# Conditioning vectors of a diffusion trunk: which groups go through TensorE as rows, which are summed on VectorE, and when

## The chip, the core and the metric

The kernel runs on one core of a Trainium2 chip. The core has TensorE (PE, matrix products), VectorE (DVE), ScalarE (ACT), GpSimd (POOL) and SyncE (SP, which issues most of the DMAs). Each engine works through its own list of instructions in order; semaphores make one engine wait for another. The metric is the device time of one execution in microseconds (us), as the median of several.

## The reference, cut to what matters

One layer of a trunk over 2048 latent rows with a context of 256 rows, both 1024 wide. All in float32.

```
ada   = silu(c)     @ w_ada + b_ada        # 6 x 1024 numbers for the latent rows
ada_c = silu(c_ctx) @ w_ada + b_ada        # the same for the context
sh1, sc1, g1, sh2, sc2, g2 = split(ada);   csh1, csc1, ... = split(ada_c)
hc = rmsnorm(ctx) * norm_mix * (1 + csc1) + csh1        # context, 256 rows
(final forward and backward states of a gated recurrence) from hc @ w_in[:, :1536]
h  = rmsnorm(x)   * norm_mix * (1 + sc1)  + sh1         # latent, 2048 rows
o  = token_mixers(h @ w_in, starting from those states)
x  = x + g1 * (o @ w_out);  h2 = modulate(rmsnorm(x), sh2, sc2)
x  = x + g2 * conv_ffn(h2);  return rmsnorm(x)
```

What matters here is the beginning: 2048 of the 6144 conditioning columns (shift sh1 and scale sc1) are needed, for the latent stream and for the context, before anything can be modulated. The others come later in the kernel, and the change doesn't touch them.

## The kernel before, in words

Activations are kept transposed, features on the 128 partitions and positions along the free axis, in 8 blocks of 128 features (`NK` = 8). To keep float32 accuracy, a product is made from a high and a low part of each operand: `split` copies to float32r on ScalarE (line 120) and subtracts on VectorE or GpSimd (line 121), and three products go into one PSUM bank (`mm3`).

**Conditioning.** `w_ada` has one shift and one scale per feature, 1024 columns each. They are cut in four groups of 512: groups 0 and 1 are the lower and upper half of the shift, groups 2 and 3 those of the scale. Index `w` is 0 for the latent stream, 1 for the context. Two ways of working a group out stand side by side:
- as rows: `ada_products` multiplies the two columns of `cs2` (silu of c and of c_ctx) with a 128x512 piece of `w_ada`, eight times into one bank (2 partitions x 512); `ada_columns` adds the bias on VectorE, and transposes the result to columns, 4 x (128 x 2).
- as sums: `ada_sums` runs on VectorE, acc = w_ada piece x scalar + acc over all 128 partitions, eight times for each `w`; a product with a matrix of ones (line 65, tile `acc` as the stationary operand) then adds over the partitions and transposes at once.

Before, groups 0, 2 and 3 are rows, group 1 is summed for both `w`, two accumulators by turns. `put_ada` writes the columns into `s1` (shift) and `a1` (norm_mix x (1 + scale)), at lines 286 and 288.

**Context and first banks.** The two context tiles (128 x 1024) are squared on ScalarE and scaled on VectorE (`x_square`, `x_scale`), transposed on TensorE into four PSUM banks (`pct`), and modulated block by block: `ctx_mod` takes scale and shift on VectorE from PSUM (line 232), the high part on ScalarE, the low part on GpSimd (blocks 0 to 3) or VectorE (4 to 7). All this stands inside `tc.manual_schedule()`, where the written order is the order on every engine. Behind it a planner orders the instructions by its own estimates.

`run_banks` then makes column blocks of `w_in`: a bank is 8 x 3 products of one 128-column block (`hi`, `lo`, split from `raw`) with 256 context columns (`chl`, `cll`) or 512 latent ones (`xh`, `xl`). Two split weights are held at a time, three raw ones. PSUM has three buffers for such banks (tag "pj"). Of a head's three context banks two are forget gates, whose `sink` applies two sigmoids on ScalarE (lines 514, 515) into the tile `cS` or `cf`, and one is the value (line 555). Between products `slot()` runs steps that have fallen due in two pumps, `hg_q` and `bg_q`. `bg_q` starts with `x_start`: squares of four latent tiles (line 221), their scaling (line 227), and `x_first`, which transposes and modulates 512 rows in 8 blocks (line 232, high part line 120, low part line 121 by turns on GpSimd and VectorE), twice. The tiles `xl` and `xh` take the memory in which the conditioning weights (`wa`) lay.

The planner's result around the change: six context banks (two heads), then banks over the latent rows and the other context banks, mixed.

Of the kernel before, what the change touches and what calls it, by code (L numbers as in the profile page):

```python
# [72 lines left out]
def tile_trunk(ctx, tc, x, c, cx, c_ctx, w_ada, b_ada, norm_mix, norm_ffn, w_in, hg_norm, sgu_g, sgu_b,  # L73
# [104 lines left out]
    with es1:  # L178
# [13 lines left out]
        def bank(tag):  # L192
            return ps.tile([P, 512], F32, tag=tag, name=tag, bufs={"pj": 3, "sc": 2, "mi": 3}[tag])
# [55 lines left out]
        acc = ph.tile([P, 2, 512], F32, tag="S", name="acc")  # L249
        G.memset(acc, 0.0)  # L250

        def load_ada(g, qs=(0, 1)):

            for q in (qs,) if isinstance(qs, int) else qs:
                t = wa[g // 2][:, 4 * (g % 2) + 2 * q:4 * (g % 2) + 2 * q + 2, :]
                wts[g, q] = t.rearrange("p a (b e) -> p (a b) e", e=512)
                ld(wts[g, q], wv[:, 4 * q:4 * q + 4, g * 512:(g + 1) * 512])

        def load_bias(g, tag):
            rows[g] = pm.tile([2, 512], F32, tag=tag, name="rows", bufs=2)  # L260
            ld(rows[g], b_ada[0:1, g * 512:(g + 1) * 512].broadcast_to([2, 512]))
# [6 lines left out]

        def ada_columns(g):
            V.tensor_add(rows[g], rows[g], pa.pop(g)[:2, :])  # L270
            pv = bank("pj")
            for j in range(4):
                T.transpose(pv[:, 2 * j:2 * j + 2], rows[g][:, j * P:(j + 1) * P], ident[:2, :2])
            put_ada(g, [pv[:, w:8:2] for w in range(2)])

        def ada_sums(k0, k1):
            for k in range(k0, k1):
                for w in range(2):
                    V.scalar_tensor_tensor(out=acc[:, w, :], in0=wts[1, k // 4][:, k % 4, :], scalar=cs2[:, k, w:w + 1],
                                           in1=acc[:, w, :], op0=ALU.mult, op1=ALU.add)  # L280

        def put_ada(g, cols):
            sl = slice(4 * (g % 2), 4 * (g % 2) + 4)
            for w in range(2):
                if g < 2:
                    V.tensor_copy(s1[:, w, sl], cols[w])
                else:
                    V.scalar_tensor_tensor(out=a1[:, w, sl], in0=cols[w], scalar=1.0, in1=nmix[:, sl],
                                           op0=ALU.add, op1=ALU.mult)
# [4 lines left out]
        def ctx_mod(k, eng):  # L294
            x_mod(pct[k // 2][:, (k % 2) * 256:(k % 2) * 256 + 256], 1, k, chl[:, k, :], cll[:, k, :], CTX, eng)
# [4 lines left out]
        with tc.manual_schedule():  # L300
# [3 lines left out]
            vr = pm.tile([50, P], F32, tag="gu", name="vr", bufs=2)  # L304
            for a, n, r0 in ((norm_mix[0], 8, 0), (norm_ffn[0], 8, 8), (hg_norm[0], 4, 16), (sgu_g[0], 4, 20),
                             (sgu_b[0], 4, 24), (conv_b[0], 22, 28)):
                S.dma_start(vr[r0:r0 + n, :], a.rearrange("(r p) -> r p", p=P))
            load_bias(2, "ot")
            for q in range(2):
                load_ada(0, q)  # L310
                load_ada(1, q)
            load_bias(0, "ot")
            for w in range(2):
                ld(acc[0:1, w, :], b_ada[0:1, 512:1024])
            load_bias(3, "vv")
            load_ada(3)
            load_raw((0, CTX))
# [5 lines left out]
            pv = bank("sc")  # L323
            T.transpose(pv[:, :50], vr, ident[:50, :50])
            V.tensor_copy(vec, pv[:, :50])
            ada_products(2, 1)
            ada_columns(2)
            x_scale(xc, ss, keep=lambda i: i)
            ada_sums(0, 4)
            ada_products(0, 0)  # L330
# [4 lines left out]
            load_raw((HW, CTX))  # L335
            ada_products(0, 1)
            ada_columns(0)
            ada_sums(4, 5)
            for k in range(4):
                ctx_mod(k, G)  # L340
                if k == 1:
                    ada_sums(5, 6)
            ada_products(3, 0)
# [3 lines left out]
            ada_sums(6, 8)  # L347
            nxt[0, CTX] = split_w((0, CTX), G)
            ada_products(3, 1)
            pz = bank("pj")  # L350
            for w in range(2):
                for j in range(4):
                    o = 2 * (4 * w + j)
                    T.matmul(pz[:, o:o + 2], acc[:, w, j * P:(j + 1) * P], ones[:, :2], start=True, stop=True)
            ada_columns(3)
            put_ada(1, [pz[:, 8 * w:8 * w + 8:2] for w in range(2)])
            for k in range(4, NK):
                ctx_mod(k, V)
            nxt[HW, CTX] = split_w((HW, CTX), V)
        xl = p1.tile([P, NK, TH], F32R, tag="xl", name="xl", align_bytes=AL)  # L360
        xh = p1.tile([P, NK, TH], F32R, tag="xh", name="xh", align_bytes=AL)

        def x_first(g0, xs):
            for k in range(NK):
# [116 lines left out]
        def run_banks(banks, peek=None):  # L481
# [3 lines left out]
            for i, (col, n0, n, sink, pre) in enumerate(banks):  # L485
# [10 lines left out]
                pj = bank("pj")  # L496
                sl = slice(n0, n0 + n)
                for k in range(NK):
# [99 lines left out]
        def marked(g, what):  # L598
# [7 lines left out]
                (view(cf, 0, [[CTX, 2], [1, CTX]]), view(cf, 2 * CTX, [[CTX, 2], [1, CTX]]), view(cb, CTX, [[1, CTX]]))]  # L606
        bg_q.add(marked(x_start(), "x0b"))
# [1135 lines left out]
```

## Time and profile before

| | us |
|---|---|
| median of 3 runs | 2509.79 (2508.38 to 2512.24) |
| the profiled execution | 2513.77 |
| its span, first to last instruction | 2511.9 |
| TensorE busy | 2440.4 (97% of the span) |
| VectorE busy | 1796.9 (72%) |
| mean granted clock of TensorE | 0.993 |

How to read the lines that follow: a group or timeline line gives start and length (us), engine, line of the kernel, operation, out<-in, shapes, a count (x8: eight merged into one entry), and in brackets the idle time before it with what ended it. PEld is the loading of TensorE's stationary operand, "SPq" the issue of DMAs by SyncE.

### The profile page before, as it was taken

What the parts mean: (1) busy time and instruction counts of PE and PEld (TensorE: products, weight loads), DVE (VectorE), ACT (ScalarE), POOL (GpSimd) and SP (SyncE); (2) the same over time, 40 slices, a digit from 0 to 9 for tenths busy, and PEclk for the clock granted to TensorE, in tenths of its full rate; (3) what the DMA queues carried; (4) which work ended last, traced back from release to release, by engine and by line L of the source; (5) the groups of instructions that cost most, each with busy time, mean ns of one, the idle gap of its engine ahead of it and who ended that gap; (6) DMA issues with size and microseconds to landing.
All of it is one profiled execution on the core that took longest, in us unless ns stands there. A gap on an engine that the chain in (4) does not pass through costs nothing.

```text
span 2511.9 us, 32816 instructions
## 1 busy us (share of the span) xinstructions
PE 2440.4 (97%) x11859; PEld 2015.6 (80%) x11859; DVE 1796.9 (72%) x2375; ACT 964.2 (38%) x1606; POOL 1062.2 (42%) x871
## 2 busy tenths in 40 slices
PE   7999999899999999999999999999999999999998
PEld 4787888788888888788788888878788888888786
DVE  5866875645766766465798877759999983767775
ACT  2554334433444443354443333333333333332252
POOL 1344232332343443100688788777777860000002
PEclk8999999999999999999999999999999999999999
DMA  8356446573354323768822222562222238835544
GB/s 293 97 185 189 133 128 193 175 250 126 106 176 143 118 97 104 257 211 255 298 86 80 88 88 87 176 227 83 84 90 92 91 122 341 298 118 182 182 151 172
DMA packets 307838, 400.13 MB, mean 159 GB/s; under 512 B 33105, under 2 KB 216137, under 8 KB 304605
## 3 DMA queue, kind: packets, MB, share of 16 engines
q1 hardware_dynamic: 304420, 397.30, 47.5%
q8 instruction: 94, 1.54, 0.3%
q10 hardware_dynamic: 3257, 0.75, 0.1%
q14 instruction: 67, 0.55, 0.1%
HBM read 288.85 MB, written 109.13 MB: 158 GB/s over the span
## 4 chain that ended last, share of the span: by engine, by line
PE 38%; DVE 7%; DMA 2%; POOL 2%; issue 2%; ACT 1%; SPq 0%; POOLq 0%; DVEq 0%; ACTq 0%
PE up L65 24%; PE dn L65 14%; DVE dn L1331 3%; DMA sT<-wd 1%; POOL Al L121 1%; DVE edges L1336 1%; DVE gp L1407 0%; DMA raw<-in_w_up_dram 0%; DVE mhl L121 0%; POOL raw L1158 0%; DMA yl<-yd 0%; DVE odd L1611 0%; POOL fl L1154 0%; DMA xn<-cv 0%; DVE tl L121 0%
## 5 line engine op out<-in xcount | busy, mean ns | idle before, releaser
L1331 DVE SCALAR_TENSOR_TENSOR dn<-gp,taps,dn 128x1024 f32<-128x1024 f32 x352 | 448.2, 1280 | 20.7 <-ACT dn L1328 17.4
L121 POOL TENSOR_TENSOR Al<-raw,Ah 128x512 fp32r<-128x512 f32 x264 | 344.9, 1313 | 99.7 <-ACT Ah L120 93.1
L65 PE MATMUL pj<-xh,whi 128*128 128x512 f32 x896 | 363.8, 406 | 0.5 <-ACT xh L120 0.5
L65 PE MATMUL dn<-th,mhl 128*128 128x512 f32 x1120 | 353.0, 396 | 5.2 <-DVE odd L1677 4.8
L65 PE MATMUL pj<-xl,whi 128*128 128x512 f32 x896 | 350.7, 392 | 1.8 <-DVE xl L121 1.1
L65 PE MATMUL pj<-xh,wlo 128*128 128x512 f32 x896 | 350.8, 391 | 1.0 <-DVE wlo L121 1.0
L65 PE MATMUL up<-xah,Ah 128*128 128x512 f32 x704 | 277.1, 394 | 1.7 <-ACT Ah L120 1.7
L65 PE MATMUL up<-xah,Al 128*128 128x512 f32 x704 | 276.4, 393 | 2.4 <-POOL Al L121 2.4
L65 PE MATMUL up<-yl,Ah 128*128 128x512 f32 x704 | 274.6, 390 | 2.1 <-DMA yl<-yd 2.1
L120 ACT CAST Ah<-raw 128x512 fp32r<-128x512 f32 x264 | 160.5, 618 | 295.3 <-PE up L65 238.8
L65 PEld LDWEIGHTS dn<-th,mhl 128*128 128x128 f32 x1120 | 212.0, 189 | 54.8 <-issue 4.6
L121 POOL TENSOR_TENSOR wlo<-raw,whi 128x1024 fp32r<-128x1024 f32 x56 | 136.8, 2442 | 250.3 <-ACT whi L120 228.2
L113 POOL TENSOR_SCALAR rs<-ss 128x2 f32<-128x2 f32 (+1 forms) x16 | 8.2, 512 | 535.4 <-ACT jk L1603 368.9
L65 PE MATMUL dn<-tl,mhl 128*128 128x512 f32 x560 | 220.9, 394 | 0.0
L65 PE MATMUL up<-yh,Ah 128*128 128x512 f32 x528 | 208.2, 395 | 0.0
L65 PE MATMUL up<-yh,Al 128*128 128x512 f32 x528 | 206.9, 392 | 0.0
L65 PE MATMUL up<-xal,Ah 128*128 128x512 f32 x528 | 205.6, 389 | 0.0
L65 PEld LDWEIGHTS pj<-xh,wlo 128*128 128x128 f32 x896 | 168.3, 188 | 37.2 <-DVE wlo L121 1.7
L65 PEld LDWEIGHTS pj<-xh,whi 128*128 128x128 f32 x896 | 168.8, 188 | 33.9 <-issue 3.5
L65 PEld LDWEIGHTS pj<-xl,whi 128*128 128x128 f32 x896 | 168.9, 188 | 32.9 <-DVE xl L121 2.1
L65 PE MATMUL dn<-wo,o 128*128 128x512 f32 x768 | 183.1, 394 | 1.5 <-DVE nt L673 0.9
L65 PEld LDWEIGHTS dn<-wo,o 128*128 128x128 f32 x768 | 141.9, 188 | 31.2 <-issue 1.1
(320 smaller groups left out, 4673.5 us busy)
## 6 DMA issues: line engine op xcount, KB each, us to landing
raw<-in_w_up_dram SPq DMA_DIRECT2D x88, 512.0 KB
mr<-m SPq DMA_DIRECT2D x85, 512.0 KB
raw<-in_w_in_dram SPq DMA_DIRECT2D x68, 512.0 KB
sT<-wd SPq DMA_DIRECT2D x88, 256.0 KB
raw<-in_w_ada_dram SPq DMA_DIRECT2D x32, 512.0 KB
m<-cv SPq DMA_DIRECT2D x22, 544.0 KB
raw<-in_w_down_dram SPq DMA_DIRECT2D x22, 512.0 KB
wd<-raw SPq DMA_DIRECT2D x22, 512.0 KB
```

The source lines that it names most:

```text
L65: return self.engine.matmul(out, lhsT, rhs, **kw)
L113: keep(G.tensor_scalar(out=r[:, :n], in0=ss, scalar1=scale, scalar2=bias, op0=ALU.mult, op1=ALU.add))
L120: keep(S.copy(hi, raw))
L121: (eng or G).tensor_sub(lo, raw, hi.bitcast(F32))
L1331: V.scalar_tensor_tensor(out=cr, in0=gt[:, t // 3:t // 3 + RH, t % 3:t % 3 + GW], scalar=taps[:, t * NF + f:t * NF + f + 1], in1=cr, op0=A ...
L1336: V.scalar_tensor_tensor(out=e[:, 0, :], in0=gt[:, 1, t % 3:t % 3 + GW], scalar=taps[:, t * NF + f:t * NF + f + 1], in1=e[:, 0, :], op0=AL ...
```

## The change

Groups 0 and 2, the lower halves, stay rows. Groups 1 and 3, the upper halves, are both summed on VectorE, each with an accumulator of its own, first for the context alone. The bias no longer comes in by loads of its own; it is loaded with the other vectors (`vr`, 66 rows now) and added as columns (`bc`). The row of a group goes from PSUM to SBUF on ScalarE (`ada_rows`). TensorE makes the first half of group 0 ahead of the transposes of group 2. Context blocks 0 to 3 are modulated on ScalarE from PSUM, blocks 4 to 7 on both engines; the low part is always VectorE's. The first weight is split early, on VectorE, and the first context bank gets its products of blocks 0 to 3 (`ctx_products`) before the sums of group 3; `run_banks` goes on with block 4. The latent stream's sums of groups 1 and 3 are put off: six steps (`last_sums`) become due in `hg_q` from 3 us on at 2.5 us distance, and `x_first` runs what is left of them before its first block. The accumulators take the memory tagged "S" (later `cS`) and "bst" (later `cb`).

```diff
+        acc = {1: ph.tile([P, 2, 512], F32, tag="S", name="acc1"),
+               3: view(ph.tile([P, NCH + 1, P], F32, tag="bst", name="acc3"), 0, [[512, 2], [1, 512]])}
...
+        def ada_rows(g, tag):
+            rows[g] = pm.tile([2, 512], F32, tag=tag, name="rows", bufs=2)
+            S.copy(rows[g], pa.pop(g)[:2, :])
...
-        def ada_sums(k0, k1):
+        def ada_sums(g, w, k0, k1):
             for k in range(k0, k1):
-                for w in range(2):
-                    V.scalar_tensor_tensor(out=acc[:, w, :], in0=wts[1, k // 4][:, k % 4, :], scalar=cs2[:, k, w:w + 1],
-                                           in1=acc[:, w, :], op0=ALU.mult, op1=ALU.add)
+                s_ = V.scalar_tensor_tensor(out=acc[g][:, w, :], in0=wts[g, k // 4][:, k % 4, :], scalar=cs2[:, k, w:w + 1],
+                                            in1=acc[g][:, w, :], op0=ALU.mult, op1=ALU.add)
+                if w == 0:
+                    pin(s_)
+        def ada_ones(g, w, to, o):
+            for j in range(4):
+                T.matmul(to[:, o + 2 * j:o + 2 * j + 2], acc[g][:, w, j * P:(j + 1) * P], ones[:, :2], start=True, stop=True)
+            put_ada(g, to[:, o:o + 8].rearrange("p (j u) -> p u j", u=2)[:, :1, :], w, w + 1)
...
+            dst = (s1, a1)[g // 2][:, w0:w1, sl]
+            V.tensor_add(dst, cols, view(bc, 4 * g, [[0, w1 - w0], [1, 4]]))
+            if g > 1:
+                V.tensor_mul(dst, dst, view(vec, sl.start, [[0, w1 - w0], [1, 4]]))
...
+        def ctx_mod(k):
+            pt = pct[k // 2][:, (k % 2) * 256:(k % 2) * 256 + 256]
+            sc, sh = a1[:, 1, k:k + 1], s1[:, 1, k:k + 1]
+            fl = pm.tile([P, 512], F32, tag="sig", name="xfl", bufs=2)
+            if k < 4:
+                S.activation(fl[:, :CTX], pt, AF.Identity, bias=sh, scale=sc)
+                S.copy(chl[:, k, :], fl[:, :CTX])
+            else:
+                S.activation(chl[:, k, :], pt, AF.Identity, bias=sh, scale=sc)
+                V.tensor_scalar(out=fl[:, :CTX], in0=pt, scalar1=sc, scalar2=sh, op0=ALU.mult, op1=ALU.add)
+            V.tensor_sub(cll[:, k, :], fl[:, :CTX], chl[:, k, :].bitcast(F32))
+        def ctx_products(c, ks):
+            hi, lo, _ = nxt[c, CTX]
+            pj = opened[c, CTX]
+            for k in ks:
+                mm3(pj[:, :CTX], hi[:, k, :], lo[:, k, :], chl[:, k, :], cll[:, k, :], k == 0, False)
...
+            load_ada(0)
+            load_raw((0, CTX))
+            load_ada(1)
             load_ada(3)
-            load_raw((0, CTX))
+            load_raw((HW, CTX))
...
             ada_products(2, 1)
+            ada_rows(2, "ot")
+            x_scale(xc, ss, keep=lambda i: i)
+            ada_products(0, 0)
             ada_columns(2)
...
+            nxt[0, CTX] = split_w((0, CTX), V)
...
             ada_products(0, 1)
+            ada_rows(0, "ot")
+            ada_sums(1, 1, 0, 8)
             ada_columns(0)
+            ada_ones(1, 1, small, 256)
+            opened[0, CTX] = bank("pj")
             for k in range(4):
+                ctx_mod(k)
+            ctx_products(0, range(4))
...
+            ada_sums(3, 1, 0, 8)
+            ada_ones(3, 1, small, 288)
             for k in range(4, NK):
-                ctx_mod(k, V)
+                ctx_mod(k)
             nxt[HW, CTX] = split_w((HW, CTX), V)
+        last_sums = []
+        for g in (1, 3):
+            last_sums += [lambda g=g, k=k: ada_sums(g, 0, k, k + 4) for k in (0, 4)]
+            last_sums.append(lambda g=g: ada_ones(g, 0, bank("mi"), 0))
...
         def x_first(g0, xs):
+            while last_sums:
+                sums_now()
...
+        for i in range(6):
+            hg_q.later(sums_now, 3.0 + 2.5 * i)
```

80 lines of the change are left out of this document (26 added, 54 removed).

## The prediction

> **What bounds the kernel now.** I read the page first, then busy time by stage, the engines' timelines up to 110 us, and who waits for whom.
>
> ```profile
> PE 2440.4 (97%) x11859; PEld 2015.6 (80%) x11859; DVE 1796.9 (72%) x2375; ACT 964.2 (38%) x1606; POOL 1062.2 (42%) x871
> 0.00:20.00 20.00, 12.08 (x28) 2.36 (x29) 2.61 (x7) 3.79 (x6) 2.69 (x11) 1.00 0.90 332
> 20.00:40.00 20.00, 14.29 (x50) 4.53 (x48) 16.78 (x24) 2.57 (x5) 6.92 (x5) 0.96 1.05 377
> 40.00:60.00 20.00, 18.76 (x104) 17.46 (x104) 10.29 (x23) 10.53 (x21) 0.24 (x2) 0.70 0.52 168
> 60.00:80.00 20.00, 16.50 (x117) 14.18 (x115) 18.62 (x28) 13.94 (x25) 11.25 (x6) 1.00 0.42 124
> 80.00:100.00 20.00, 17.44 (x103) 13.68 (x102) 17.81 (x30) 7.26 (x15) 6.33 (x6) 1.00 0.24 64
> 49.90:104.90 55.00, 47.62 (x299) 39.81 (x298) 46.89 (x73) 31.05 (x59) 19.59 (x13) 0.97 0.38 115
> ```
>
> Columns of a stage: its length, then busy time of PE, PEld, DVE, ACT, POOL, the granted clock, the DMA share, GB/s. TensorE bounds the whole (97%), so an edit in the first stage counts only by how far it shifts the moment from which TensorE no longer stops. Up to 40 us TensorE waits for data and conditioning; from 60 to 100 us it idles again, 3.5 and 2.6 us in the two stages, and there VectorE is the full engine (18.6 and 17.8 of 20). From 49.9 to 104.9 VectorE is busy 46.9 of 55 us. The waits say what its 8.1 us of idle are:
>
> ```profile
> DVE wlo L121 <- ACT whi L120: 4.7, 3, 2.7
> DVE xfl L232 <- POOL xl L121: 1.3, 2, 0.9
> DVE xg L227 <- POOL rs L115: 0.9, 1, 0.9
> DVE xl L121 <- ACT xh L120: 0.7, 1, 0.7
> DVE xfl L232 <- PE mi L69: 0.5, 1, 0.5
> ```
>
> ```profile
> 50.10 1.23 DVE L121 TENSOR_TENSOR wlo<-raw,whi 128x1024 fp32r<-128x1024 f32 x1 [0.52 <-ACT whi L120]
> 61.05 2.74 DVE L227 TENSOR_SCALAR xg<-xg,rs 128x1024 f32<-128x1024 f32 x4 [0.91 <-POOL rs L115]
> 64.84 1.52 DVE L232 TENSOR_SCALAR xfl<-mi,a,s 128x512 f32<-128x512 f32 x2
> 104.21 0.69 DVE L121 TENSOR_TENSOR xl<-xfl,xh 128x512 fp32r<-128x512 f32 x1
> 108.45 0.28 PE L65 MATMUL pj<-ch,whi 128*128 128x256 f32 x1
> ```
>
> So one VectorE stream runs from the second weight split (50.10) over normalising and modulating the first 1024 latent rows to their last low part (104.21, done 104.90), and TensorE enters the next context bank 3.6 us behind it, at 108.45. In both programs as built, the instruction order of every engine is the same from about there on. The change is worth what it moves that point.
>
> **The change: the front.** These rows price it.
>
> ```profile
> 12.72 3.60 PE L65 MATMUL pj<-wa,cs 128*2 128x512 f32 x8
> 20.95 1.53 PE L69 MATMUL mi<-ident,raw 128*128 128x128 f32 x12
> 22.84 3.60 PE L65 MATMUL pj<-wa,cs 128*2 128x512 f32 x8
> 28.92 7.03 PE L65 MATMUL pj<-wa,cs 128*2 128x512 f32 x16
> 39.51 3.54 PE L65 MATMUL pj<-ones,acc 128*128 128x2 f32 x16 [3.56 <-POOL wlo L121]
> 269.52 0.95 PE L65 MATMUL mi<-ones,acc 128*128 128x2 f32 x8
> 22.56 5.39 DVE L279 SCALAR_TENSOR_TENSOR acc<-wa,cs,acc 128x512 f32<-128x512 f32 x8 [3.48 <-DMA acc<-in_b_ada_dram]
> 327.66 3.10 DVE L885 SCALAR_TENSOR_TENSOR acc<-raw,cs,acc 128x512 f32<-128x512 f32 x4
> 34.36 5.71 DVE L279 SCALAR_TENSOR_TENSOR acc<-wa,cs,acc 128x512 f32<-128x512 f32 x4
> 36.07 2.79 POOL L121 TENSOR_TENSOR wlo<-raw,whi 128x1024 fp32r<-128x1024 f32 x1
> 33.77 0.40 ACT L120 CAST ch<-xfl 128x256 fp32r<-128x256 f32 x1 [1.84 <-DVE xfl L232]
> L1205 ACT ACTIVATE fl<-up,s,a x56: 543/558/568, 1043.5 to 1205.6; 128x256 f32<-128x256 f32 x56
> ```
>
> Removed: 7.03 us of TensorE products for group 3 (28.92), at a place where TensorE then waits 3.56 us anyway, and POOL's share in the front, which stretched VectorE's last four sums to 5.71. Added: sixteen more sums (32 instead of 16) and sixteen more transposing products with ones.
>
> The sums alternated between two accumulators before: 8 in 5.39, 0.67 each. Now eight in a row add to the same accumulator. A chain like that is the row at 327.66: 4 in 3.10, 0.775 each, so eight cost 6.2. The Trainium skill (VectorE: DVE Perf Modes, "The DRAIN you can't avoid") says that a semaphore between chained VectorE instructions costs nothing extra; by that eight would again take 5.4, and my total would be 2.1 us lower. The trace differs, and it decides.
>
> TensorE: group 2 ends at 16.3 as before; group 0's first half (3.6, the length of its second at 22.84) now follows at once, to 19.9; columns 0.3; sixteen context transposes 1.9 (20.95 to 22.84) to 22.1; second half to 25.7, ScalarE's copy of the row and its transposes to 26.9. VectorE: group 2's columns at 20.8, the first weight's low part 1.2, then group 1's sums 22.0 to 28.2. The loads, in slices of 2.5 us:
>
> ```profile
> GB/s 6 228 402 417 391 393 407 410 408 409 392 315 306 402 411 370 261 377 13 0 5 286 275 130 328 29 143 181 105 0 37 173 206 4 0 7 0 0 175 124
> 48.14 0.54 DVE L232 TENSOR_SCALAR xfl<-sc,a,s 128x256 f32<-128x256 f32 x1
> 47.80 0.42 DVE L121 TENSOR_TENSOR cl<-xfl,ch 128x256 fp32r<-128x256 f32 x1 [0.47 <-ACT ch L120]
> ```
>
> On SP's queue now come group 2 and the context (3.1 MB), group 0 (2.1), the first weight (0.5), group 1 (2.1) and group 3 (2.1). The slices add up to 7.9 MB at 23 us and 10 MB at 28.5; a transfer lands about 1 us behind its bytes. So group 1's second half is there at 24, its fifth sum starts at 25; group 3's is needed after 32. The second and third weights wait for the two context tiles (free at 22.1) behind group 3, which delays nothing, as the queue is that long anyway; the latent rows follow and land before 40, long before their squares. The five bias loads taken off SP and the one put on ScalarE's queue (SP's second load of group 2 now waits on an early small one) hide behind that stream, which keeps at 400 GB/s; if they don't, the front slips by a small load's landing, some 2 us. Then ScalarE modulates four blocks: 0.56 for scale and shift from PSUM (L1205's form, same shape) and 0.40 for the cast, chained 0.93 with VectorE's subtraction behind: 3.7 + 0.5. It starts at 28.4 if it waits for its own shift columns alone, or at 29.5 if also for group 1's (eight products with ones, warm, 0.95): VectorE is free at 32.6 or 33.7. Group 3's sums: 6.2, to 38.8 or 39.9. The twelve early products of the first context bank lie beside this. The ones products find TensorE idle for five microseconds; after 3.56 us of idle the row at 39.51 shows 0.22 each, so 1.8 instead of 0.95; columns 0.4: 41.05 or 42.1. Four more blocks, scale-and-shift 0.54 and subtraction 0.42 chained on VectorE, 3.75. **The second weight split starts at 44.8 or 45.9, instead of 50.10.** I take the middle, 45.3: a lead of 4.8 us.
>
> **The change: the stage behind it.** Sixteen sums (groups 1 and 3 for the latent stream) now sit in the VectorE stream. In the built order they stand 4, 3, 1 (group 1) and 8 singly (group 3), before the first latent modulation. A chain of four costs 3.1, one of three 2.3, those between other instructions 0.7: 3.1 + 2.3 + 0.7 + 8 x 0.7 = 11.7, and three small column writes 0.4. The stream gets 46.9 + 12.1 = 59.0 busy.
>
> Its idle time, with times for the early case: before, 4.7 was waiting for ScalarE's weight casts, which wait for a bank to end. Now
>
> ```profile
> 51.38 0.39 PE L65 MATMUL pj<-ch,wlo 128*128 128x256 f32 x1 [0.76 <-DVE wlo L121]
> 55.22 0.32 PE L65 MATMUL pj<-ch,whi 128*128 128x256 f32 x1
> 50.22 0.38 ACT L514 ACTIVATE cS<-pj 128x256 f32<-128x256 f32 x1 [0.15 <-issue]
> 50.77 1.06 ACT L221 ACTIVATE xjk<-xg 128x1024 bf16<-128x1024 f32 x1
> 59.33 0.19 ACT L221 ACTIVATION_READ_ACCUMULATOR xjk<-xg 128x1 f32 x1
> 59.67 0.20 POOL L113 TENSOR_SCALAR rs<-xss 128x4 f32<-128x4 f32 x1 [20.82 <-ACT xjk L221]
> 61.86 0.33 PE L69 MATMUL mi<-ident,xg 128*128 128x128 f32 x1 [1.17 <-DVE xg L227]
> ```
>
> bank two runs from 46.05; 18 products at half clock take 3.8 (51.38 to 55.22), the bank ends at 50.4. VectorE has split bank three and done four sums by 50.25 and waits 1.3 for the next cast.
> The new wait lies in the tags: the accumulator of group 1 has taken buffer S, in which the first context gates are kept. Sink cS therefore waits until the ones products have read it, behind bank four. Banks one and two stay in PSUM, banks three and four share the one buffer left. ScalarE's queue holds behind that sink the other context sinks (0.38 each) and all four squares of the latent rows (1.06 and 0.19 to read the sum). Bank four ends at 56.65, ones at 57.9 (VectorE waits 1.05 for them), first square at 58.6 instead of 50.77. With sinks between, squares end at 63.9, POOL's rstd takes 1.5 (59.52 to 61.05 before), normalising at 65.5 instead of 61.05 (VectorE waits 0.6). Group 3's sums end at 69.9; TensorE has stood since bank six ended at 64.4, so ones are cold again, 1.8; VectorE waits 1.5; first latent modulation at 73.3 instead of 64.84. Later waits as before, 1.3 for POOL, 0.7 and 0.5 for casts and transposes: 2.6. Idle: 1.3 + 1.05 + 0.6 + 1.5 + 2.6 = 7.05.
>
> Sum: 45.3 + 59.0 + 7.05 = 111.35, against 104.90: **+6.4 us**. A second way, by the stages: first modulation +8.5 (early case), less two weight splits (2.4) now behind it, no POOL split among them: +5 to +7. I take +6.2. TensorE has 2.75 us of latent transposes more to do behind 74 us than before (five groups of four at about 0.55), but enough idle there: 2.6 in the stage from 80 alone. The profiled execution is 2513.77 for a span of 2511.9, 4.0 above the median of 2509.79: it would become 2520.0, and the median **2516**.
>
> Bounds: the lead of the front is at least 4.2 (45.9) and at most 6.4 (unchained sums 1.6 less, 0.67 each); added work at least 16 x 0.67 = 10.7 and at most 16 x 1.43 (34.36) = 22.9, were POOL beside every sum; it is beside few, so I stay near the first. The idle could be 2.6 (all new waits covered) to 10.
>
> **Rivals.** (a) The idle swallows more: new waits overlap with sums that the stream had to do anyway, idle 3.5, chain spacing 0.67. Then -1 to +4, 2512. For: the scheduler spread the sums. Against: each wait named has nothing ahead of it in VectorE's order.
> (b) Faster: the latent modulation isn't what TensorE needs next, and the lead stays. Bank two's split products start 4.9 earlier (51.38 to 46.5) and the stall of 1.17 at 61.86 vanishes: -6, 2504. It decides if the stream ends by 99.9, that is if VectorE's idle of 8.1 takes in nearly all twelve added. Against: 4.7 of it came at bank ends, in pieces under 2.7, and the latent squares start eight late.
> (c) POOL beside the sums: the fourth split of POOL and its power (2.4 and 1.06) fall at 64 to 70, among the last sums, and each costs VectorE about its own length, as 34.36 against 36.07 shows (5.71 instead of 3.10, beside 2.79). In the sum this replaces a like collision before; where it comes on top, +3.5: 2519.5. The Trainium skill (SBUF — State Buffer, "Who interferes with whom") has it as an exclusive lock between VectorE with two SBUF inputs and GpSimd: the second blocks for the whole instruction. The trace agrees: 2.6 more beside 2.79.
>
> **Numbers.** 0.2% is 5.0 us, about what a measurement of this kernel tells from no change. Forecast, +4 to +8.5: 0.50, of which 0.42 lies above 5.0. (a) 0.27, (b) 0.08, (c) and worse 0.15. Slower 0.42 + 0.15 = 0.57, same 0.08 + 0.27 = 0.35, faster 0.08. Range 2509 to 2521.5: it leaves out (b) and the ends of (a) and (c), about 0.17.
>
> **What would show it.** Right: second weight split near 45; first cS sink behind 56; TensorE idle for about 5 us before the second set of ones near 64 to 70; first modulation of latent rows behind 70; the bank of 108.45 near 114.5. Wrong: latent squares that start before 55, sums that hide in VectorE's idle, or a first modulation before 67; in the front, a split at 42 or at 48.

## The result and the profile after

The changed kernel takes 2522.42 us (median, 2516.81 to 2524.07) where the kernel before takes 2509.79 in the same series: ratio 1.0042, 95% interval 1.0028 to 1.0056. That is slower, by some 10.5 us as the ratio has it (7 to 14); the two medians lie 12.6 apart. The profiled execution took 2516.81 us for a span of 2515.0. It is the fastest of its series, so the two spans are no measure of the change; the shift of matching instructions is.

Busy time by stage of the changed kernel, with the columns of the table before (length, PE, PEld, DVE, ACT, POOL, granted clock, DMA share, GB/s); the last row is the VectorE stream, from the second weight split to the last low part of the latent rows:

```profile
0.00:20.00 20.00, 13.04 (x25) 2.30 (x25) 1.94 (x6) 4.62 (x8) 3.57 (x12) 1.00 0.89 315
20.00:40.00 20.00, 12.33 (x58) 7.68 (x56) 15.16 (x25) 4.95 (x10) 0.00 (x0) 0.75 1.06 392
40.00:60.00 20.00, 16.96 (x99) 15.10 (x98) 15.47 (x25) 8.36 (x13) 0.00 (x0) 0.74 0.65 206
60.00:80.00 20.00, 14.06 (x77) 13.31 (x78) 17.40 (x28) 9.30 (x20) 5.99 (x4) 0.68 0.39 114
80.00:100.00 20.00, 17.48 (x94) 14.16 (x92) 15.13 (x27) 11.51 (x23) 6.83 (x6) 0.89 0.09 27
46.31:114.02 67.71, 56.71 (x313) 48.39 (x314) 57.60 (x93) 30.53 (x58) 17.18 (x13) 0.84 0.31 94
```

TensorE, the bound of the whole, idles longer: it is busy for 14.06 us between 60 and 80, against 16.50 before, and at a granted clock of 0.68 against 1.00. Along the timeline of the changed kernel:

```profile
46.31 1.23 DVE L121 TENSOR_TENSOR wlo<-raw,whi 128x1024 fp32r<-128x1024 f32 x1
59.73 1.06 ACT L221 ACTIVATE xjk<-xg 128x1024 bf16<-128x1024 f32 x1
66.76 2.74 DVE L227 TENSOR_SCALAR xg<-xg,rs 128x1024 f32<-128x1024 f32 x4 [0.91 <-POOL rs L115]
68.83 2.87 POOL L121 TENSOR_TENSOR wlo<-raw,whi 128x1024 fp32r<-128x1024 f32 x1 [2.11 <-ACT whi L120]
69.42 2.83 DVE L283 SCALAR_TENSOR_TENSOR acc<-wa,cs,acc 128x512 f32<-128x512 f32 x1
73.26 1.84 PE L65 MATMUL mi<-ones,acc 128*128 128x2 f32 x8 [5.86 <-DVE acc L283]
76.55 1.52 DVE L232 TENSOR_SCALAR xfl<-mi,a,s 128x512 f32<-128x512 f32 x2
113.35 0.67 DVE L121 TENSOR_TENSOR xl<-xfl,xh 128x512 fp32r<-128x512 f32 x1
117.92 0.28 PE L65 MATMUL pj<-ch,whi 128*128 128x256 f32 x1
```

The second weight split starts 3.8 us earlier than before (46.31, 50.10), the first square of the latent rows 9.0 later (59.73, 50.77), the first latent modulation 11.7 later (76.55, 64.84), the stream's last low part 9.1 later (113.35, 104.21), and TensorE enters the bank that serves as landmark 9.5 later (117.92, 108.45). Behind the landmark the order of instructions is the same in both kernels. The later end is made ahead of it.

### The profile page after: what moved, and what is told of

It is laid out like the page before. It is cut to its first block, busy times and chain, and to the rows that moved or that the text cites. A ratio compares the mean times of both kernels' runs of the same rounds, so it can differ in the third digit from the quotient of the medians.

```text
span 2515.0 us, 32819 instructions
## 1 busy us (share of the span) xinstructions
PE 2442.0 (97%) x11855; PEld 2023.4 (80%) x11855; DVE 1804.0 (72%) x2392; ACT 968.1 (38%) x1612; POOL 1053.4 (42%) x867
```

## The experiments

Four theories were told apart. A: the deferred sums' own VectorE time, ahead of the first latent modulation, sets it. B: the accumulator's buffer, which holds up the cS sink and with it the squares, sets it. C: POOL's split beside a sum adds about 2 us. D: the front gains or loses it. Each result is read at the landmark (108.45 before, 117.92 after) and by the ratio to the kernel before. The front's end moves by up to 2.5 us between executions of the same front (the second split was at 46.31 in the changed kernel and at 47.98 in a kernel that differs from it only behind that point, and at 48.05 and 50.52 in two kernels that differ only in a buffer; the last section shows what moves it). There is one profile of each kernel. Distances from the second split are therefore the surer reading.

**The sums left out.**

```diff
         for g in (1, 3):
-            last_sums += [lambda g=g, k=k: ada_sums(g, 0, k, k + 4) for k in (0, 4)]
             last_sums.append(lambda g=g: ada_ones(g, 0, bank("mi"), 0))
```

> The changed kernel with the 16 deferred sums left out: the latent rows' upper shifts and scales are then the bias alone (that part of the computation is left out); their products with the ones stay. The landmark is the context bank that ended at 108.45 us before and at 117.92 us after. Theory A (the sums' own VectorE time sets the later end): they are busy 11.9 us in the changed kernel, and the one stretched by POOL 2.1 of it, so the landmark comes 10 to 12 us earlier, at 106 to 108, and the time is at or below the kernel before. Theory B (the wait of the cS sink for the accumulator's buffer sets it): the products with the ones still stand behind bank four only if bank four's time holds them; without sums they can run at once, so the squares of the latent rows start near 51 instead of 59.73 and the first latent modulation comes near 65: the landmark is near 106 to 108 too. The two differ in the next two runs. Theory D (the front): the second split stays at 46.3 us, and the landmark must be earlier than the kernel before by at most the 3.8 us of lead that the front has: not below 104.6.

Ratio 1.0002 (0.9993 to 1.0011), landmark 108.18. The slowdown is gone. But the products with the ones had nothing left to wait for and were planned into the front, where VectorE waited for them (1.91 and 1.85 us); the second split came at 49.57 instead of 46.3. So this run shows that the sums are the cause, and not what the front's lead is worth. (The sums are busy for 14.03 us in the changed kernel; the 11.9 of the expectation leaves out the 2.1 by which one of them was stretched.)

**The accumulator in another buffer, all sums kept.**

```diff
-        acc = {1: ph.tile([P, 2, 512], F32, tag="S", name="acc1"),
+        acc = {1: view(ph.tile([P, NCH + 1, P], F32, tag="fs", name="acc1"), 0, [[512, 2], [1, 512]]),
```

> The changed kernel with the group-1 accumulator in the memory of tag fs (used by a later bank) instead of tag S, so that the cS sink no longer waits for the products with the ones. All sums stay. Theory A: only idle time is gained, the sums still stand ahead of the first latent modulation on VectorE; first sink near 53 instead of 59.2, squares near 53 instead of 59.73, but the first modulation (76.55) not before 73, and the landmark at 115 to 116.5 (1.5 to 3 us earlier than 117.92), the time 1.005 to 1.002 of the kernel before. Theory B: the squares, the rstd and the modulation all come 6 to 8 us earlier, landmark at 110 to 112, the time within 0.1% of the kernel before. The stretched sum beside POOL's split (theory C) may go or stay, worth up to 2.1 us.

Ratio 1.0033 (1.0021 to 1.0046), landmark 118.44. From the timeline of this run:

```profile
49.40 1.06 ACT L221 ACTIVATE xjk<-xg 128x1024 bf16<-128x1024 f32 x1
58.26 2.74 DVE L227 TENSOR_SCALAR xg<-xg,rs 128x1024 f32<-128x1024 f32 x4 [0.91 <-POOL rs L115]
76.27 0.74 DVE L283 SCALAR_TENSOR_TENSOR acc<-wa,cs,acc 128x512 f32<-128x512 f32 x1
79.99 1.66 DVE L232 TENSOR_SCALAR xfl<-mi,a,s 128x512 f32<-128x512 f32 x2 [0.60 <-PE mi L69]
60.00:80.00 20.00, 9.82 (x68) 9.44 (x69) 17.61 (x33) 4.18 (x8) 2.45 (x1) 0.80 0.45 132
```

The squares start 10.3 us earlier than in the changed kernel and the rows are normalised 8.5 earlier, and nothing comes of it, not even the 1.5 to 3 us that theory A allowed: the last sum still starts at 76.27, the modulation at 79.99, and TensorE is busy for 9.82 of the 20 us ahead of that. The gate levels (VectorE's short steps on `cS` and `tot`, lines 497 and 504), released early, only took VectorE's turns between the sums. With sixteen sums deferred, theory B falls: its wait was covered by the sums.

**Both edits at once.** The two diffs above.

> Both edits at once: the 16 deferred sums left out (the latent rows' upper shifts and scales are then the bias alone) and the accumulator in the other memory. If the buffer costs nothing without the sums, this agrees with the run without sums alone within 0.5 us at the landmark; theory B expects a further gain of 2 us or more over it. Either way this is what the front alone is worth: the second split at 46.3 us against 50.10 is 3.8 us of lead, so the landmark is at 104.7 to 106 if the lead is kept and near 108 if the stretch behind swallows it.

Ratio 1.0006 (0.9997 to 1.0015), landmark 108.46, second split 49.99: as without the sums alone. Without sums the buffer costs nothing.

**No sums and no products with ones.**

```diff
-        for g in (1, 3):
-            last_sums += [lambda g=g, k=k: ada_sums(g, 0, k, k + 4) for k in (0, 4)]
-            last_sums.append(lambda g=g: ada_ones(g, 0, bank("mi"), 0))
+        for t in (s1, a1):
+            V.tensor_copy(t[:, 0, 4:8], t[:, 1, 4:8])
...
```

> The changed kernel without the deferred sums and without their products with the ones; the latent rows take the context's upper shifts and scales instead (their own are left out: two copies of four columns in their place). Unlike the run that only left the sums out, nothing is put into the front, so the second split should stand at 46.5 to 47 us. The runs so far: first latent modulation 64.84 before (second split 50.10), 64.52 without the sums (49.57), 64.72 with rows for group 3 (49.02), 76.55 in the changed kernel and 79.99 with the other buffer; landmark 108.45, 108.18, 108.58, 117.92, 118.4. Theory A (what stands ahead of the first latent modulation sets the landmark, and the deferred sums stand there): the modulation near 62 to 63, landmark 104.5 to 106, that is 12 to 13 us earlier than the changed kernel, and the time some 3 us below the kernel before. If the stretch between swallows the front's lead (TensorE's banks at half clock set the squares, and these the modulation): modulation at 64.5, landmark at 108, the time of the kernel before.

Ratio 1.0004 (0.9994 to 1.0013), second split 47.97, first modulation 63.90, landmark 107.81. Against the changed kernel this prices the sixteen sums together with their products with the ones, for which VectorE waits 1.2 and 1.7 us there: from second split to landmark 59.84 us here, 71.61 there, 11.8 more. It also shows that a lead of the front mostly does not come through: 2.13 us at the split (the front was expected a microsecond earlier, at 46.5 to 47), 0.64 at the landmark. The front loses nothing by itself, so theory D falls as the cause of the later end.

**Eight sums deferred instead of sixteen.** Group 3 goes back to rows on TensorE; the latent column of group 1 alone is deferred.

```diff
-            ada_sums(3, 1, 0, 8)
-            ada_ones(3, 1, small, 288)
+            ada_products(3, 0)
+            ada_products(3, 1)
+            ada_rows(3, "ot")
+            ada_columns(3)
...
-        for g in (1, 3):
+        for g in (1,):
             last_sums += [lambda g=g, k=k: ada_sums(g, 0, k, k + 4) for k in (0, 4)]
```

> Group 3 as rows on TensorE (behind the products of blocks 0 to 3, second split near 49), and only the latent column of group 1 deferred: 8 sums instead of 16, the accumulator in the same buffer as in the changed kernel. 16 deferred sums moved the landmark from 107.8 (none deferred) to 117.9. If every deferred sum costs its own time (0.78 us of VectorE): half of it, landmark 112.5 to 113.5, time 1.002. If VectorE's idle time in the bank stage (5.65 us of it between 50 and 58 us in the kernel before) takes the first 8 and only what is over costs: landmark 108.5 to 110, time 1.000 to 1.001. The cS sink behind the products with the ones puts the squares at 56 to 58; if these set the modulation: modulation 68 to 70, landmark 111 to 112.

Ratio 1.0031 (1.002 to 1.0042), landmark 115.80, above all that was expected: more than half the cost for half the sums. The squares started at 62.12 and the first modulation at 74.94. Here the chain over the buffer is the longer one, which the next run tests, with the accumulator in tag "fs".

```diff
-        acc = {1: ph.tile([P, 2, 512], F32, tag="S", name="acc1")}
+        acc = {1: view(ph.tile([P, NCH + 1, P], F32, tag="fs", name="acc1"), 0, [[512, 2], [1, 512]])}
```

> The run with 8 deferred sums (group 1 alone, group 3 as rows) once more, with the accumulator in the memory of tag fs, so that the cS sink does not wait for the products with the ones. With the accumulator in tag S it had its squares at 62.12 us, its first latent modulation at 74.94 and its landmark at 115.80, more than half of what 16 sums cost. With all 16 sums the other buffer gained nothing (118.44 for 117.92). If with 8 sums it is the buffer that sets the end: squares near 51, modulation 65 to 67, landmark 108.5 to 110.5, time 1.000 to 1.001. If the sums' own VectorE time does, here too: modulation 70 to 72, landmark 112.5 to 114.5, time 1.002.

Ratio 1.0025 (1.0016 to 1.0035), squares 52.86, modulation 71.27, landmark 114.45, but with the second split at 50.52 instead of 48.05. From split to landmark it is 63.93 us against 67.75: the buffer is worth 3.8 us. The first modulation waited for the sums now:

```profile
67.62 0.74 DVE L282 SCALAR_TENSOR_TENSOR acc<-wa,cs,acc 128x512 f32<-128x512 f32 x1
69.79 0.95 PE L65 MATMUL mi<-ones,acc 128*128 128x2 f32 x8
70.78 0.16 DVE L295 TENSOR_TENSOR s<-mi,bc 128x4 f32<-128x4 f32 x1 [1.14 <-PE mi L65]
```

So theory B accounts for 3.8 of the 9.4 us that eight sums cost between split and landmark, and for nothing with sixteen, and VectorE's idle time did not take in eight sums either: 63.93 is 5.6 more than the 58.35 of the kernel before. Modulation, landmark and time fall where the sums' own time was expected to put them; measured from the split, both causes show.

**The eighth weight split on VectorE.** POOL's split beside the sums is taken away.

```diff
-            split(hi, lo, raw, eng or (V if w_n[0] < 8 or w_n[0] < 20 and w_n[0] % 2 else G))
+            split(hi, lo, raw, eng or (V if w_n[0] < 9 or w_n[0] < 20 and w_n[0] % 2 else G))
```

> The changed kernel with the eighth split of a weight on VectorE (1.22 us) instead of POOL (2.87 us, which stood beside the one sum that took 2.83 us instead of 0.77). Theory C (the collision): the sum is short again, VectorE gains 2.1 us and gives 1.2 back, so the second products with the ones come near 72.4 instead of 73.26 and the landmark near 117.0; what POOL did elsewhere stays. If nothing waited on that sum: landmark 118 to 119. In neither case is the time told apart from the changed kernel's (1.003 to 1.005 of the kernel before).

Ratio 1.0036 (1.0023 to 1.0048). The sum in question took 0.75 us again instead of 2.83. From split to landmark 70.72 against 71.61: 0.9 less, which is the 2.1 gained minus the 1.2 for the split. Theory C is right in its place and its size, and small; the front was 1.7 us late in this execution, so the landmark itself (118.70) shows nothing.

**The context blocks modulated as before.**

```diff
-                ctx_mod(k)
+                x_mod(pct[k // 2][:, (k % 2) * 256:(k % 2) * 256 + 256], 1, k, chl[:, k, :], cll[:, k, :], CTX, V)
```

(in both loops)

> The changed kernel with the eight context blocks modulated as in the kernel before (VectorE multiplies and adds, ScalarE casts, VectorE subtracts), all else as changed: the ScalarE part of the change undone. A block takes about 1.36 us that way, and VectorE comes to group 3's sums some 2.5 us later: second split near 49 instead of 46.31. If the front's lead never reached the landmark: 117.5 to 119, as in the changed kernel. If it did, with the sums behind it: 120.5 to 121, time 1.005.

Ratio 1.0057 (1.004 to 1.0073), second split 51.16, landmark 123.46, both later than expected. Here the split is 4.85 us later than in the changed kernel and the landmark 5.5: with the sums behind it, a microsecond of the front counted in full in this pair, as it would with VectorE as the bound from the front to the landmark. Of the 4.85, 0.8 is not ScalarE's part: the first products with the ones took 1.84 us in this execution and 1.02 in the changed kernel's. ScalarE's part of the change was thus worth some 4.7 us inside a change that lost 9.5.

**Group 3 as rows, nothing deferred: three orders.** First behind the context's products of blocks 0 to 3:

```diff
-            ada_sums(3, 1, 0, 8)
-            ada_ones(3, 1, small, 288)
+            ada_products(3, 0)
+            ada_products(3, 1)
+            ada_rows(3, "ot")
+            ada_sums(1, 0, 0, 8)
+            ada_columns(3)
+            ada_ones(1, 0, small, 320)
...
```

(In this kernel and the three behind it the deferred steps and group 3's accumulator are taken out as well.)

> Group 3 goes back to rows on TensorE, in the stretch of 29.8 to 39.2 us in which TensorE does little, and VectorE takes the second column of group 1 (8 sums of 0.78 us) in the place of group 3's; no sum is left behind the front. All else is as in the changed kernel. The cold products with the ones ahead of blocks 4 to 7 (1.84 us) are replaced by four transposes; second split near 44.5 us (46.31 after, 50.10 before). Theory A with the lead kept: landmark near 103 (5.5 us earlier than before), time 2504, ratio 0.998. If the stretch behind swallows the lead because its squares or loads come no earlier: landmark 106 to 108, ratio 0.999 to 1.000. Theory D (the front itself costs, ScalarE's and VectorE's turns on the blocks): landmark above 108.

Ratio 0.9998 (0.9989 to 1.0007), second split 49.02, landmark 108.58. The rows ran from 33.97 to 42.33, and VectorE idled 4.07 us for their columns.

Then ahead of those products:

```diff
             ada_columns(0)
+            ada_products(3, 0)
             ada_ones(1, 1, small, 256)
+            ada_sums(1, 0, 0, 8)
+            ada_products(3, 1)
+            ada_rows(3, "ot")
+            ada_columns(3)
+            ada_ones(1, 0, small, 320)
...
```

> Group 3 as rows on TensorE again, but ahead of the context's products (in two halves, the ones of group 1 between them), and VectorE sums both columns of group 1 one after the other; nothing is deferred. In the first form of this edit the rows stood behind the products of blocks 0 to 3 and took 33.97 to 42.33 us, so that the second split was at 49.02. Here the rows end near 36.5, the context's blocks are modulated from about 37.5, and the second split is at 44 to 46.5 us (before 50.10). Theory A with the lead kept: first latent modulation 60 to 62, landmark 103 to 105, the time 3 to 5 us below the kernel before (ratio 0.998 to 0.999). Lead swallowed by the bank stage: landmark 107 to 108.5, ratio 1.000.

Ratio 0.9988 (0.9979 to 0.9997), but second split 49.19 and landmark 108.91, 0.5 us later than before. What the time gained is not to be seen at the landmark, and behind it the order is the same; I don't count it as shown. The next kernel dealt the blocks out in turn:

```diff
             for k in range(4):
                 ctx_mod(k)
+                x_mod(pct[k // 2 + 2][:, (k % 2) * 256:(k % 2) * 256 + 256], 1, k + 4, chl[:, k + 4, :], cll[:, k + 4, :], CTX, V)
...
-            for k in range(4, NK):
-                ctx_mod(k)
```

> As the kernel before this one in the list (rows for group 3 ahead, nothing deferred), with the eight context blocks dealt out alternately: blocks 0 to 3 by ScalarE alone, and between them blocks 4 to 7 by VectorE with ScalarE's cast, as the kernel before has it, so that the two engines never read one PSUM tile at a time. Eight blocks then take about 6 us instead of 8.6 (ScalarE 4 x 0.97 + 4 x 0.41 = 5.5 us; VectorE 4 x 0.55 + 8 x 0.43 = 5.6 us): second split 42 to 44.5. Lead kept: landmark 101 to 103, ratio 0.997 to 0.998. Lead swallowed: landmark 107 to 108.5.

Ratio 1.0007 (0.9997 to 1.0017), second split 49.58, landmark 109.46. The two missed their split by 2.7 and 5.1 us (later than the end of the expected range) through their own order: VectorE waited 4.84 and 3.36 us for the products with the ones ahead of the second column's sums, and in the second of them the blocks waited for each other, 2.25 us a pair. The last form mends both: group 1's second sums ahead of the first ones products, and the blocks one step apart.

```diff
-            ada_ones(1, 1, small, 256)
             ada_sums(1, 0, 0, 8)
+            ada_ones(1, 1, small, 256)
...
+                V.tensor_scalar(out=fl[:, :CTX], in0=pt, scalar1=a1[:, 1, j:j + 1], scalar2=s1[:, 1, j:j + 1], op0=ALU.mult, op1=ALU.add)
+                both[k]()
+                S.copy(chl[:, j, :], fl[:, :CTX])
+                if k < 3:
+                    both.append(ctx_mod(k + 1))
+                V.tensor_sub(cll[:, j, :], fl[:, :CTX], chl[:, j, :].bitcast(F32))
...
```

(`both` holds the low-part subtractions of blocks 0 to 3)

> Rows for group 3 ahead of the context's products and nothing deferred, as in the two runs before, but with their two mistakes of order mended: VectorE's second column of group 1 now stands ahead of the wait for the first products with the ones (it cost 4.84 us of idle time, 29.5 to 34.3), and blocks 0 to 3 on ScalarE and 4 to 7 on VectorE are overlapped by one step, with a buffer of their own, so that a pair takes 1.4 to 1.6 us instead of 2.25. The blocks start near 37.5 and end near 44; second split 43 to 44.5 (before 50.10). So far a second split of 49.57, 49.02, 47.97 and 49.19 gave a landmark of 108.18, 108.58, 107.81 and 108.91: a lead of up to 2.1 us came through by 0.64 at most. If the lead is only lost because these leads were small against the half clock: landmark 103 to 105, time 0.997 to 0.999. If the bank stage sets its own pace (TensorE's matmuls at half clock, 0.21 us each, six banks of 24): first latent modulation 62.5 to 64, landmark 106.5 to 108, time 0.999 to 1.000.

Second split 44.25, landmark 105.51, ratio 0.9993 (0.9982 to 1.0004). The landmark lies between the two expectations, 2.9 us earlier than in the kernel before, half of the front's lead of 5.85. The time is not told from that of the kernel before. What took the other half:

```profile
48.36 1.04 ACT L120 CAST whi<-raw 128x1024 fp32r<-128x1024 f32 x1 [4.14 <-PE pj L65]
49.44 1.22 DVE L121 TENSOR_TENSOR wlo<-raw,whi 128x1024 fp32r<-128x1024 f32 x1 [3.47 <-ACT whi L120]
45.00:50.00 5.00, 5.00 (x24) 5.00 (x25) 1.20 (x3) 1.64 (x4) 0.00 (x0) 0.50 0.38 117
50.00:55.00 5.00, 5.00 (x41) 5.00 (x40) 2.45 (x6) 4.70 (x10) 0.00 (x0) 0.93 0.55 168
```

The timeline rows show the next cast waiting 4.14 us for a bank on TensorE, and VectorE waiting for the cast; the first stage row shows TensorE busy for the whole 5 us, at half clock. When nothing is deferred, the bank stage goes at TensorE's pace, and half or more of an earlier front is lost in waiting.

**All runs by time and landmark.** The ratio times 2510 against the landmark's shift from 108.45:

| kernel | deferred sums | second split | landmark | shift | by the ratio |
|---|---|---|---|---|---|
| before | 0 | 50.10 | 108.45 | 0 | 0 |
| changed | 16 | 46.31 | 117.92 | +9.5 | +10.5 |
| other buffer | 16 | 47.06 | 118.44 | +10.0 | +8.3 |
| split 8 on VectorE | 16 | 47.98 | 118.70 | +10.3 | +9.0 |
| blocks as before | 16 | 51.16 | 123.46 | +15.0 | +14.3 |
| eight sums | 8 | 48.05 | 115.80 | +7.4 | +7.8 |
| eight, other buffer | 8 | 50.52 | 114.45 | +6.0 | +6.3 |
| no sums | 0 | 49.57 | 108.18 | -0.3 | +0.5 |
| no sums, other buffer | 0 | 49.99 | 108.46 | 0 | +1.5 |
| no sums, no ones | 0 | 47.97 | 107.81 | -0.6 | +1.0 |
| rows, first order | 0 | 49.02 | 108.58 | +0.1 | -0.5 |
| rows, second order | 0 | 49.19 | 108.91 | +0.5 | -3.0 |
| rows, blocks in turn | 0 | 49.58 | 109.46 | +1.0 | +1.8 |
| last form | 0 | 44.25 | 105.51 | -2.9 | -1.8 |

The landmark's shift and the time agree within the intervals (about 2.5 to 4 us either way) in every kernel but one: the second order of the rows, whose interval (-5.3 to -0.8) leaves out its landmark's +0.5. The cause of that one is open.

## Why the prediction came out as it did

The direction, the mechanism and the landmark were right; the size was too small, 9.5 us at the landmark for 6.2. The median of 2522.42 lies 0.9 above the range's upper end; 2509.79 times the ratio is 2520.3, inside it. Among the prediction's cases, +10.5 lies in "(c) and worse" (0.15) and not in its own +4 to +8.5 (0.50), though the interval from 7 on reaches into that. Point by point:

- **The bound.** Right. What the change was worth was made ahead of the named bank; the table shows the time following it, within the intervals, in all kernels but one.
- **The front.** Lead 3.8 us at the second split instead of 4.8, below the 4.2 that was given as its least. The sums took what the chained row gave (8 in 6.25, 6.2 forecast), the cold ones 1.84 (1.8), and blocks 0 to 3 started at 28.75, as the earlier of the two cases had it. The term that was mis-sized is the last four blocks: 3.75 us, reckoned as VectorE's own time. They took 4.8 (41.50 to 46.31), because ScalarE and VectorE both read a block's PSUM tile and wait for each other; the rest is half a microsecond at the columns and that the forecast took the middle of its two cases. Luck is in it too: the first products with the ones, reckoned as warm (0.95), took 1.02 here and 1.83 or 1.84 in six of the nine other kernels that have the same order up to there, so that the lead of the same front was only 3.0 with the other buffer and 2.1 with split 8 on VectorE. From the timelines of VectorE and ScalarE in the changed kernel:

```profile
42.10 0.55 DVE L313 TENSOR_SCALAR xfl<-mi,a,s 128x256 f32<-128x256 f32 x1 [0.64 <-ACT ch L312]
42.68 0.56 ACT L312 ACTIVATE ch<-mi,s,a 128x256 fp32r<-128x256 f32 x1 [0.61 <-DVE xfl L313]
44.78 0.57 ACT L312 ACTIVATE ch<-sc,s,a 128x256 fp32r<-128x256 f32 x1 [1.07 <-DVE xfl L313]
```

The Trainium skill (PSUM — Partial Sum Buffer, "PSUM bank collisions raise a hardware error") says that no two engines may be in the same bank and quadrant at a time, reads included, and that semaphores have to guard such accesses. The trace agrees: at 42.10 VectorE waits 0.64 us for ScalarE's `ch`, of which it uses nothing, and the forecast should have asked for this. In the last form each engine has banks of its own, and the low parts stand one step later; a pair of blocks takes 1.35 to 1.41 us there. The banks alone don't give that: in the kernel with the blocks in turn, with the same banks and without that step, a pair took 2.25.

- **The chained sums.** 0.78 each, as the row of the trace had it and not as the Trainium skill's rule (VectorE: DVE Perf Modes, "The DRAIN you can't avoid") would have made it, 5.4 for eight. The measurement decides.
- **The stream.** Start 45.3, busy 59.0, idle 7.05: 111.35. Measured, 46.31 + 57.60 + 10.11 = 114.02. Busy came out 1.4 lower although the sums took 14.03 instead of 11.7; POOL was busy beside the stream for 17.18 us instead of 19.59, and other instructions were stretched less (below). Idle came out 3.1 higher, the largest miss and just over the 10 given as its most, and not where the new waits were; that busy and idle erred in opposite directions was luck. The stage rows of the stream, split at the first latent modulation (76.55; before, 64.84), show where. First the changed kernel's:

```profile
46.31:76.55 30.24, 23.07 (x146) 22.21 (x147) 25.38 (x38) 13.17 (x24) 4.53 (x3) 0.78 0.47 140
76.55:114.02 37.47, 33.64 (x169) 26.18 (x168) 32.22 (x57) 17.36 (x34) 12.65 (x10) 0.89 0.18 56
```

Then the part behind the modulation in the kernel before:

```profile
64.84:104.90 40.06, 34.95 (x213) 27.94 (x212) 37.31 (x60) 20.60 (x39) 18.34 (x11) 1.00 0.31 93
```

Ahead of the modulation VectorE idles 4.86, and 4.45 was forecast. Behind it 5.25, where the forecast took 2.6 over from the kernel before. There VectorE has 32.22 us to do where it had 37.31. Two weight splits (2.4 us) that stood behind the modulation before now stand ahead of it, and two instructions that ran beside POOL's take 0.62 and 0.68 us instead of 2.11 and 1.72. From the timelines of VectorE and POOL in the kernel before:

```profile
66.42 1.22 DVE L121 TENSOR_TENSOR wlo<-raw,whi 128x1024 fp32r<-128x1024 f32 x1
74.63 1.21 DVE L121 TENSOR_TENSOR wlo<-raw,whi 128x1024 fp32r<-128x1024 f32 x1
76.96 2.40 POOL L121 TENSOR_TENSOR wlo<-raw,whi 128x1024 fp32r<-128x1024 f32 x1
77.76 2.11 DVE L470 TENSOR_TENSOR cf<-cf 128x256 f32<-128x256 f32 x1
79.31 1.56 POOL L121 TENSOR_TENSOR xl<-xfl,xh 128x512 fp32r<-128x512 f32 x1
79.69 1.72 DVE L121 TENSOR_TENSOR xl<-xfl,xh 128x512 fp32r<-128x512 f32 x1
```

VectorE's waits behind the modulation, in the changed kernel, with total, count and longest:

```profile
DVE xfl L232 <- POOL xl L121: 2.0, 2, 1.5
DVE xl L121 <- ACT xh L120: 1.0, 1, 1.0
DVE xk L227 <- POOL rs L115: 0.9, 1, 0.9
DVE hf L618 <- ACT cdh L617: 0.9, 1, 0.9
DVE sgt L972 <- ACT sig L971: 0.4, 1, 0.4
```

The last three do not occur there before, and the first two were 1.3 and 0.7. So "later waits as before" is the step that failed: they cost 2.65 us more. That the work which had covered them was gone is argued from the order; no run tests it alone. The other kernels fit in part: behind the modulation VectorE idles 6.3 us (other buffer) and 6.6 us (eight sums) with one split left there, and 2.7 (eight, other buffer) and 4.9 (split 8 on VectorE) with two.
- **The buffer.** The wait came as named: first sink 59.18, first square 59.73 (58.6 forecast). It did not set the end: with the other buffer the squares were 10.3 us earlier and the landmark no earlier. The forecast's chain over the squares was thus right in its times and not the cause; with half the sums it would have been a part of it.
- **First modulation.** 73.3 forecast, by the early case of the front (split at 44.8), 76.55 measured: 1.5 from the front, 2.1 from the one sum that POOL's split stretched, which the forecast had only in rival (c), less 0.35 elsewhere.
- **Rivals.** (a), more idle swallowed, fell: idle grew to 10.11. (b), the lead kept, fell: it needed nearly all of the sums to hide, and 11.8 us of them showed. Even with no sums deferred a lead of 2.13 came through by 0.64. (c) came true in part: one sum beside POOL's split took 2.83 for 0.75; the sum beside the power kept its 0.75. The run without it gave 0.9 us back. The Trainium skill's lock (SBUF — State Buffer, "Who interferes with whom") fits that row.
- **From the landmark to the time.** +9.5 at the landmark and +10.5 by the ratio (7 to 14) agree.

The miss at the landmark, 9.5 for 6.2, adds up: 1.0 from the front, 3.1 of idle less 1.4 of busy time, 0.35 between the stream's end and the bank (3.90 us for 3.55), and 0.25 by which the sum was rounded down. The remaining 1.0 by the ratio is not resolved by the measurement.

## What to carry to other kernels

Moving work out of a stage that waits for data into one where an engine is nearly full can cost its whole length: here 11.8 us for sixteen sums of 0.75, although that engine showed 8 us of idle time; the idle time moved along with the waits behind it and was 10.1 us in the end. A lead won in front of a stage counted in full where the same engine stayed the bound behind it (5.5 for 4.85) and by half at most where another one set the pace (2.9 of 5.85, 0.64 of 2.13, nothing of 1.08 and 0.91), so ask first who paces the stage behind. And before a new wait is called the cause, ask whether the work beside it is longer: freeing the buffer gained nothing with sixteen sums and 3.8 us with eight, measured from the second split.

## What the runs showed of the hardware that was not expected

- TensorE's clock added to what a late load cost. The kernel with split 8 on VectorE has the changed kernel's front; the first weight landed 1.1 us later there (its cast starts at 20.85 for 19.75). The stage from 28 to 30 us and the products with the ones, first of the changed kernel and then of that one:

```profile
28.00:30.00 2.00, 1.14 (x9) 1.17 (x9) 0.79 (x4) 1.22 (x3) 0.00 (x0) 0.96 1.09 378
28.86 1.02 PE L65 MATMUL sc<-ones,acc 128*128 128x2 f32 x8 [1.45 <-DVE s L296]
```

```profile
28.00:30.00 2.00, 0.19 (x1) 0.22 (x2) 1.59 (x4) 0.30 (x1) 0.00 (x0) 0.85 1.07 384
29.81 1.84 PE L65 MATMUL sc<-ones,acc 128*128 128x2 f32 x8 [2.65 <-DVE s L296]
```

In both the granted clock falls to 0.50 ahead of 30 us. One kernel has its products just ahead of the fall, 1.02 us, the other behind it, 1.84. The sums end 0.96 later there, the second split 1.67. It takes no late load: with the other buffer the products start at 28.90, only 0.04 later than in the changed kernel, and take 1.84 as well. TensorE had finished the row products ahead of them a microsecond sooner (25.3 for 26.3), and the clock had fallen sooner: 0.90 from 26 to 28 us, 0.50 from 28 to 30.
- Once down, the clock stayed down for a while although TensorE worked: 0.50 from 45 to 50 us in the last form, with TensorE busy for all 5 us, and 0.93 from 50 to 55.
- A single sum of 0.75 us took 2.83 beside POOL's split of 2.87: it started 0.59 us into the split and ended 0.55 behind it (72.25, 71.70), as if it had waited for the whole of what was left.
